# Two-layer hybrid decoder trunk: a one-column product as tensor_scalar, a planner with other prices, and work moved between engines

## The chip, the cores and the metric

The kernel runs on one core of a Trainium2 chip. The metric is the device time of one execution in microseconds; three runs stand for a kernel, and their median is quoted. The engines are TensorE (PE in the profile; PEld is its weight load), VectorE (DVE), ScalarE (ACT), GpSimd (POOL) and SyncE (SP), which issues all DMAs.

## What is computed

Two decoder layers on 1024 tokens of width 1024 in float32, with RMSNorm before and after every sub-layer. Layer 0 mixes with an HGRN2 recurrence (4 heads) beside a chunked gMLP (4 channel groups); layer 1 with dilated sliding-window attention (16 heads). Each layer ends with a squared-ReLU feed-forward of 4096. The parts that the change touches:

```python
def rmsnorm(x, g):
    y = xf * lax.rsqrt(jnp.mean(xf * xf, axis=-1, keepdims=True) + EPS)
    return (y * g.astype(F32)).astype(x.dtype)
...
# gMLP, inside chunks of 128 positions, W_s causal
v = layernorm(v, ln_g, ln_b)
mixed = jnp.einsum('gts,bnsgc->bntgc', w, vb) + b_s.T[None, None, :, :, None]
return u * mixed
...
# HGRN2, per head
o = rmsnorm(o, norm_g.reshape(A_HEADS, A_DV))
o = o.reshape(b_, s_, A_WIDTH) * jax.nn.silu(g)
...
# attention: every head runs (128,1), (512,4), (2048,16) and merges them
mask = (dist >= 0) & (dist <= W) & (k_pos >= 0)
```

## The kernel before, in words

The program is not issued in the order in which it is written. Every call goes to a recorder (Plan.record, Plan.add), which stores it as a numbered operation with its dependences and an estimated cost (Plan.cost). At the end Plan.run replays all operations as a list scheduler: each engine has a queue of what is ready and takes the operation with the lowest number; an operation that becomes ready later runs after its due time. Each engine executes its instructions on the chip in the order that the plan emitted them, so estimated costs decide the order of every queue, but not the work. For VectorE the plan adds a delay where an operation is marked "pair" (two inputs in SBUF) and GpSimd is still busy in the plan. Nearly every instruction of the trace bears line 422, the emitting line; groups are told apart by tile and shape. Tiles come from pools (name "b" in the trace); HT holds activations, WP weights, and mm, tr, pa, pb are banks of PSUM. Values used in products are split in a high and a low part, copied by ScalarE and subtracted by VectorE or GpSimd, and multiplied as three fast products.

The stages, by the trace: input norms and the projection of layer 0 (to about 75 us), HGRN2 heads with the other projections as filling (to 330), output projection and norms (to 475), the first feed-forward product in sixteen blocks (to 780), the second one in four stages of eight chunks (to 1105), attention of layer 1 (to 1575), its output projection (to 1665), and the feed-forward of layer 1 (first product to 2005, second to the end).

The parts that the change touches:

- rstd_act (line 658) and newton (669) compute reciprocal roots on one column per token tile: rstd_act once for every norm of 1024, 64 times in all; newton in three steps, for each of eight tiles of the gMLP norm (one column) and of the HGRN2 head norm (four columns). The last product is a tensor_tensor.
- consts0 (766) prepares constants of layer 0, among them the transposed mixing matrices wsT and the bias, each in a plain form and one with reversed order. lng, lnb and anr are rows broadcast to all partitions.
- gmlp_norm (949) normalizes on VectorE and applies gain and bias on GpSimd (two operations of 128x512 a tile); gmlp_mix (963) multiplies with the mixing matrix and adds the bias on VectorE in two halves.
- onorm (975) multiplies by the root for all four heads at once on VectorE, then by the gain on GpSimd.
- attn_mask (1093) builds a quarter of the attention mask, 256 columns, in a single tile x, with four index generations and sixteen operations on GpSimd and two on VectorE, and stores it to DRAM (maskd); ff2 calls it after chunks 3 to 6 of layer 0. layer1_mix loads the whole mask before attention.
- Attention leaves its output in oTd with the tokens of each tile of 128 in the order (r, u), r being the position modulo 4. reload_oT (1351) restores the order by reading in steps of four.
- ff2 (1572) makes, per chunk, the differences of weight halves on GpSimd (128x1024), splits hidden values and weights on ScalarE and VectorE, two chunks ahead of the products.
- post_end (1761) loads the residual tile, adds the normed result, and stores the tile: in halves for the final output, otherwise at once.

Of the kernel before, what the change touches and what calls it, by code (L numbers as in the profile page):

```python
# [8 lines left out]
F32 = mybir.dt.float32  # L9
# [3 lines left out]
AF = mybir.ActivationFunctionType  # L13
OP = mybir.AluOpType
# [3 lines left out]
P = 128  # L18
D = 1024
# [11 lines left out]
NEG = -1.0e30  # L31
# [145 lines left out]
class Plan:  # L177
# [79 lines left out]
    def add(self, calls):  # L257
# [3 lines left out]
        o["pair"] = any(sum(isinstance(x, View) and x.buf.n not in self.inpsum and x.shape[-1] > 1  # L261
                            for x in list(a)[1:] + [kw.get("in0"), kw.get("in1")]) > 1 for _, _, a, kw in calls)
# [34 lines left out]
    def cost(self, o, eng, meth, a, kw):  # L297
# [31 lines left out]
        return 147 + (2.15 if meth == "tensor_tensor" else 3.3 if meth == "tensor_scalar" else 1.2) * n  # L329
# [14 lines left out]
    def run(self):  # L344
# [81 lines left out]
        while left:  # L426
# [29 lines left out]
            else:  # L456
                end = at + o["cost"]
                if e == "DVE" and o["pair"]:
                    end += min(max(free.get("POOL", 0.0) - at, 0.0), max(o["cost"], 700.0))
# [25 lines left out]
class Trunk:  # L485
# [172 lines left out]
    def rstd_act(self, ss):  # L658
# [7 lines left out]
        nc.vector.tensor_tensor(r, y, z, op=OP.mult)  # L666
        return r

    def newton(self, t, y, n, steps):
        V = self.nc.vector  # L670
        for _ in range(steps):
# [8 lines left out]
            V.tensor_tensor(y2, y, z, op=OP.mult)  # L680
# [85 lines left out]
    def consts0(self, pool):  # L766

        nc, a = self.nc, self.a
        with nc.pool() as tp:
# [36 lines left out]

            ge = tp.tile([P, P], F32, name="ge")
# [7 lines left out]
            for back in range(2):  # L815
# [10 lines left out]
                with nc.group():  # L826
                    for g in range(4):
# [4 lines left out]
                                     bs.strided(P - 1, back3) if back else bs.rearrange("p (g t) -> p g t", g=4), AF.Copy, scale=0.5)  # L832
                self.wsT.append(wt)
                self.bias.append(bias)
        self.lng = self.row(pool, a["b_ln_g"], 512, "lng")
        self.lnb = self.row(pool, a["b_ln_b"], 512, "lnb")
# [112 lines left out]
    def gmlp_norm(self, pool, o, sums):  # L949
# [9 lines left out]
        nc.gpsimd.tensor_tensor(vn, vn, self.lng, op=OP.mult)  # L959
        nc.gpsimd.tensor_tensor(vn, vn, self.lnb, op=OP.add)  # L960
        return vn

    def gmlp_mix(self, t, ob, vn):
# [7 lines left out]
        for i in range(2):  # L971
            part, bias = (x[:, 256 * i:256 * i + 256].rearrange("p (g t) -> p g t", g=2) for x in (tr, self.bias[t % 2]))
            nc.vector.tensor_tensor(ob[t // 4][i][:, :, t % 4 * P:(t % 4 + 1) * P], part, bias, op=OP.add)

    def onorm(self, pool, o):
# [8 lines left out]
        ov = o.rearrange("p (h v) -> p h v", h=4)  # L984
        nc.vector.tensor_tensor(ov, ov, r[:, :, None].to_broadcast([P, 4, P]), op=OP.mult)
        nc.gpsimd.tensor_tensor(o, o, self.anr, op=OP.mult)
# [106 lines left out]
    def attn_mask(self, pool, start):  # L1093


        G = self.nc.gpsimd
        n = 256
        for c0 in (start,):
# [5 lines left out]
            G.tensor_copy(u, d)  # L1104
            G.tensor_scalar(M, u, 128.0, None, op0=OP.is_le)
# [466 lines left out]
    def ff2(self, l, w, a, xmid, xout):  # L1572
# [86 lines left out]
        for m in range(3 * NC):  # L1659
# [27 lines left out]
            if l == 0 and 3 <= m <= 6:  # L1687
                self.attn_mask(prep, 256 * (m - 3))
# [128 lines left out]
```

## Time and profile before

| | |
|---|---|
| median of 3 runs | 2319.9 us (2319.55 to 2323.67) |
| profiled execution, its own time | 2320.68 us |
| its span | 2318.9 us |
| granted TensorE clock, mean | 0.995 |
| VectorE, ScalarE, GpSimd busy | 1616.1, 1114.1, 1097.3 us |
| DMA | 319.10 MB, 138 GB/s |

The span runs from the first to the last instruction; the execution's own time has a little around it. Busy time does not count waits on semaphores, but an engine that is held up inside an instruction counts as busy. A time in brackets behind an instruction is the idle time of its engine before it, with the engine that ended it. The chain of work that ended last runs for 75% of the span through TensorE and for 12% through VectorE.

### The profile page before, as it was taken

To read this page: it belongs to the slowest core of one execution; us is meant where nothing else is said; L and a number is where in the kernel's file an instruction comes from. 1 tells how busy PE (TensorE), PEld (TensorE's weight loads), DVE (VectorE), ACT (ScalarE), POOL (GpSimd) and SP (SyncE) were. 2 spreads that over 40 slices of the span, in tenths; PEclk is the share of its full clock that TensorE was granted. 3 is DMA by queue.
4 is the path that set the end of the run, shared out by engine and by line. 5 is a ranking of instruction groups with operands and counts; after the bars stand their busy time and mean duration, and the time that the engine had idled before them with its cause. 6 is when DMAs were issued, how large, how long until landed. Compare 5 with 4: busy or idle time off the path is not lost.

```text
span 2318.9 us, 32947 instructions
## 1 busy us (share of the span) xinstructions
PE 2259.9 (97%) x11314; PEld 1929.9 (83%) x11314; DVE 1616.1 (70%) x3106; ACT 1114.1 (48%) x2403; POOL 1097.3 (47%) x1184
## 2 busy tenths in 40 slices
PE   8999999999999998999999999998999999999998
PEld 7888778888888787887999999996788888888887
DVE  7688975665555955848888887877765555787746
ACT  6444444442222432435777777787452222433333
POOL 2121453355555889415555555543345555645204
PEclk9999999999999999999999999999999999999999
DMA  5110123334443957754311111114334443877654
GB/s 173 55 35 22 37 82 97 112 111 153 151 150 132 327 203 239 250 206 157 103 46 46 47 46 44 53 43 155 113 132 150 150 151 138 290 277 267 224 176 160
DMA packets 214768, 319.10 MB, mean 138 GB/s; under 512 B 14132, under 2 KB 99144, under 8 KB 214600
## 3 DMA queue, kind: packets, MB, share of 16 engines
q1 hardware_dynamic: 214600, 317.00, 40.5%
q8 instruction: 89, 1.46, 0.3%
q14 instruction: 79, 0.65, 0.1%
HBM read 226.24 MB, written 90.70 MB: 137 GB/s over the span
## 4 chain that ended last, share of the span: by engine, by line
PE 75%; DVE 12%; ACT 4%; POOL 3%; DMA 3%; issue 2%; SPq 0%; DVEq 0%; ACTq 0%; POOLq 0%
PE mm L422 34%; PE pa L422 20%; PE pb L422 13%; PE tr L422 9%; DVE b L422 9%; POOL b L422 3%; ACT b L422 3%; DVE WP L422 2%; DVE HT L422 1%; DMA b<-in_w_ff_dram 1%; DMA b<-in_w_in_odd_dram 1%; DMA b<-oTd 1%; DMA b<-hc 1%; ACT HT L422 0%; ACT WP L422 0%
## 5 line engine op out<-in xcount | busy, mean ns | idle before, releaser
L422 POOL TENSOR_TENSOR b<-b,b 128x512 f32<-128x512 f32 (+4 forms) x500 | 576.4, 1169 | 668.3 <-ACT b L422 324.5
L422 PE MATMUL mm<-WP,HT 128*128 128x512 f32 (+2 forms) x3744 | 822.5, 362 | 3.3 <-DVE HT L422 1.2
L422 PEld LDWEIGHTS mm<-WP,HT 128*128 128x128 f32 x3744 | 655.3, 190 | 82.1 <-DVE HT L422 2.3
L422 ACT ACTIVATE b<-b 128x512 f32<-128x512 f32 (+6 forms) x653 | 327.1, 513 | 369.8 <-POOL b L422 190.0
L422 POOL TENSOR_TENSOR b<-b 128x512 f32<-128x512 f32 (+4 forms) x368 | 331.8, 907 | 352.0 <-DVE b L422 246.0
L422 ACT ACTIVATE WP<-b 128x1024 fp32r<-128x1024 f32 (+2 forms) x248 | 194.3, 792 | 340.2 <-PE pb L422 190.5
L422 DVE TENSOR_TENSOR WP<-b,WP 128x1024 fp32r<-128x1024 f32 (+1 forms) x164 | 225.8, 1385 | 127.9 <-ACT WP L422 127.5
L422 DVE TENSOR_TENSOR b<-b,b 128x1024 fp32r<-128x1024 f32 (+6 forms) x382 | 239.3, 642 | 76.5 <-ACT b L422 58.7
L422 ACT ACTIVATE b<-mm 128x512 f32<-128x512 f32 (+3 forms) x346 | 152.6, 454 | 265.8 <-PE mm L422 246.2
L422 DVE TENSOR_TENSOR HT<-b,HT 128x1024 fp32r<-128x1024 f32 (+3 forms) x131 | 217.9, 1671 | 23.2 <-ACT HT L422 23.0
L422 PE MATMUL tr<-b,b 128*128 128x128 f32 x1074 | 171.1, 278 | 30.2 <-DVE b L422 24.2
L422 PE MATMUL pa<-WP,HT 128*128 128x512 f32 x768 | 193.8, 390 | 0.0
L422 DVE TENSOR_TENSOR b<-tr,b 64x128 fp32r<-64x128 f32 (+5 forms) x404 | 162.7, 407 | 32.8 <-ACT b L422 25.4
L422 PE MATMUL tr<-WP,HT 128*128 128x512 f32 x672 | 171.6, 392 | 7.6 <-DVE b L422 7.3
L422 ACT ACTIVATE HT<-b 128x1024 fp32r<-128x1024 f32 (+4 forms) x147 | 142.6, 973 | 73.8 <-PE mm L422 30.3
L422 PEld LDWEIGHTS tr<-b,b 128*128 128x128 f32 x1074 | 128.9, 147 | 54.1 <-DVE b L422 27.7
L422 PE MATMUL mm<-HT,b 128*128 128x512 f32 x720 | 173.7, 390 | 0.0
L422 PE MATMUL pa<-WP,b 128*128 128x512 f32 x720 | 173.6, 389 | 0.0
L422 DVE TENSOR_TENSOR b<-pa,b 128x512 f32<-128x512 f32 x110 | 75.4, 689 | 135.7 <-PE pa L422 135.6
L422 PEld LDWEIGHTS pa<-WP,HT 128*128 128x128 f32 x768 | 144.2, 188 | 29.9
L422 PEld LDWEIGHTS pa<-WP,b 128*128 128x128 f32 x720 | 134.9, 188 | 27.9
L422 PEld LDWEIGHTS mm<-HT,b 128*128 128x128 f32 x720 | 134.8, 188 | 27.8
(63 smaller groups left out, 3041.1 us busy)
## 6 DMA issues: line engine op xcount, KB each, us to landing
b<-in_w_ff_dram SPq DMA_DIRECT2D x172, 512.0 KB, 4.9
hc<-b SPq DMA_DIRECT2D x224, 256.0 KB, 2.1
b<-hc SPq DMA_DIRECT2D x112, 512.0 KB, 5.6
b<-in_w_in_odd_dram SPq DMA_DIRECT2D x64, 192.0 KB, 2.9
x<-b SPq DMA_DIRECT2D x24, 512.0 KB, 2.7
b<-x SPq DMA_DIRECT2D x24, 512.0 KB, 3.4
b<-in_w_in_even_dram SPq DMA_DIRECT2D x32, 256.0 KB, 2.8
wd<-b SPq DMA_DIRECT2D x16, 512.0 KB, 3.5
```

Of the source, the lines that this page charges most:

```text
L422: return getattr(self.real[eng], meth)(*[x.real() if isinstance(x, View) else x for x in a], **{k: x.real() if isinstance(x, View) else x ...
```

## The change

1. Planner: GpSimd's prices are changed (memset has one of its own); "pair" becomes shares(), which marks any VectorE operation without PSUM that has two inputs, or one input and more than one column of output (a number per partition counts only outside tensor_scalar). The added delay counts a further operation if GpSimd has one ready, and its cap changes.
2. The last product of rstd_act and of newton with one column is a tensor_scalar that takes its second factor as a number per partition.
3. The gMLP norm's gain and bias are no longer applied to the values. The gain becomes a number per partition in the mixing's last step (four scalar_tensor_tensor of 128x128); the bias times the row sums of the mixing matrix, by a product with ones, is added to the bias in the setup. lng and lnb are loaded as 128x4.
4. onorm does both of its products in one scalar_tensor_tensor per head, on VectorE.
5. attn_mask runs on VectorE but for the index generations, and is called after chunks 14, 16, 18 and 20.
6. reload_oT reads and writes plainly; the tokens stay in the order (r, u) in layer 1. post_end therefore loads x2 and stores the result with four DMAs of 32 partitions each (rows_of).

```diff
-        o["pair"] = any(sum(isinstance(x, View) and x.buf.n not in self.inpsum and x.shape[-1] > 1
-                            for x in list(a)[1:] + [kw.get("in0"), kw.get("in1")]) > 1 for _, _, a, kw in calls)
+        o["pair"] = any(self.shares(*c) for c in calls)
...
-        return 147 + (2.15 if meth == "tensor_tensor" else 3.3 if meth == "tensor_scalar" else 1.2) * n
+        if meth == "memset":
+            return 62 + 0.83 * n
+        return 150 + (2.4 if meth == "tensor_tensor" else 4.0 if meth == "tensor_scalar" else 1.2) * n
+
+    def shares(self, eng, meth, a, kw):
+
+        views = [x for x in list(a) + [kw.get("in0"), kw.get("in1")] if isinstance(x, View) and x.shape[-1] > 0]
+        if any(x.buf.n in self.inpsum for x in views) or meth.startswith("dma"):
+            return False
+        out = kw["out"] if "out" in kw else a[0]
+        n = sum(x.shape[-1] > 1 or meth != "tensor_scalar" for x in views if x is not out)
+        return n > 1 or n == 1 and math.prod(out.shape[1:]) > 1
...
-                    end += min(max(free.get("POOL", 0.0) - at, 0.0), max(o["cost"], 700.0))
+                    busy = max(free.get("POOL", 0.0) - at, 0.0)
+                    if busy and now["POOL"]:
+                        busy += o["cost"]
+                    end += min(busy, max(0.85 * o["cost"], 700.0))
...
-        nc.vector.tensor_tensor(r, y, z, op=OP.mult)
+        nc.vector.tensor_scalar(r, y, z, None, op0=OP.mult)
...
-            V.tensor_tensor(y2, y, z, op=OP.mult)
+            if n == 1:
+                V.tensor_scalar(y2, y, z, None, op0=OP.mult)
+            else:
+                V.tensor_tensor(y2, y, z, op=OP.mult)
...
+            self.lng, lnb = pool.tile([P, 4], F32, name="lng"), pool.tile([P, 4], F32, name="lnb")
+            for x, src in ((self.lng, a["b_ln_g"]), (lnb, a["b_ln_b"])):
+                nc.sync.dma_start(x, bass.AP(tensor=src.tensor, offset=src.offset, ap=[[1, P], [P, 4]]))
...
+                tr = self.tr_bank()
+                with nc.group():
+                    nc.tensor.matmul(tr, self.ones.bitcast(F32), wt.rearrange("p g t -> p (g t)"), start=True, stop=True)
+                for g in range(4):
+                    gs = slice(g * P, (g + 1) * P)
+                    nc.vector.scalar_tensor_tensor(bias[:, gs], tr[:, gs], lnb[:, g:g + 1], bias[:, gs], op0=OP.mult, op1=OP.add)
...
-        nc.gpsimd.tensor_tensor(vn, vn, self.lng, op=OP.mult)
-        nc.gpsimd.tensor_tensor(vn, vn, self.lnb, op=OP.add)
...
-            nc.vector.tensor_tensor(ob[t // 4][i][:, :, t % 4 * P:(t % 4 + 1) * P], part, bias, op=OP.add)
+        for g in range(4):
+            gs = slice(g * P, (g + 1) * P)
+            nc.vector.scalar_tensor_tensor(ob[t // 4][g // 2][:, g % 2, t % 4 * P:(t % 4 + 1) * P], tr[:, gs], self.lng[:, g:g + 1],
+                                           self.bias[t % 2][:, gs], op0=OP.mult, op1=OP.add)
...
-        nc.vector.tensor_tensor(ov, ov, r[:, :, None].to_broadcast([P, 4, P]), op=OP.mult)
-        nc.gpsimd.tensor_tensor(o, o, self.anr, op=OP.mult)
+        for h in range(4):
+            hs = slice(h * P, (h + 1) * P)
+            nc.vector.scalar_tensor_tensor(o[:, hs], o[:, hs], r[:, h:h + 1], self.anr[:, hs], op0=OP.mult, op1=OP.mult)
...
-            G.tensor_copy(u, d)
-            G.tensor_scalar(M, u, 128.0, None, op0=OP.is_le)
-            self.nc.vector.tensor_scalar(e, d, 3, None, op0=OP.bitwise_and)
-            G.tensor_scalar(t, e, 0, None, op0=OP.is_equal)
...
+            V.tensor_copy(u, d)
+            V.tensor_scalar(M, u, 128.0, None, op0=OP.is_le)
+            V.tensor_scalar(e, d, 3, None, op0=OP.bitwise_and)
+            V.tensor_scalar(t, e, 0, None, op0=OP.is_equal)
...
-        src = raw.rearrange("p k (r u) -> p k u r", r=4)
-        hi, lo = (self.HT[:, x, k0:k1, ts].rearrange("p k (u r) -> p k u r", r=4) for x in range(2))
-        nc.scalar.activation(hi, src, AF.Copy)
-        (nc.gpsimd if t < LAG["rel"] else nc.vector).tensor_tensor(lo, src, hi.bitcast(F32), op=OP.subtract)
+        hi, lo = (self.HT[:, x, k0:k1, ts] for x in range(2))
+        nc.scalar.activation(hi, raw, AF.Copy)
+        nc.vector.tensor_tensor(lo, raw, hi.bitcast(F32), op=OP.subtract)
+
+    def rows_of(self, x, t, cs, spread):
+
+
+        if not spread:
+            return [(slice(0, P), x[t * P:(t + 1) * P, cs])]
+        return [(slice(32 * r, 32 * r + 32), x[t * P + r:(t + 1) * P:4, cs]) for r in range(4)]
...
-            if l == 0 and 3 <= m <= 6:
-                self.attn_mask(prep, 256 * (m - 3))
+            if l == 0 and m in (14, 16, 18, 20):
+                self.attn_mask(prep, 128 * (m - 14))
...
-        nc.sync.dma_start(x, xin[rows, :])
+        for p, src in self.rows_of(xin, t, slice(0, D), xin is self.x2):
+            nc.sync.dma_start(x[p], src)
...
-                nc.sync.dma_start(xout[rows, d], x[:, d])
+                for p, dst in self.rows_of(xout, t, d, xout is self.out[0]):
+                    nc.sync.dma_start(dst, x[p, d])
```

## Rows read from the trace of the kernel before

**Rows 1.** The page, part 1: busy time, share of the span, instructions

```profile
PE 2259.9 (97%) x11314; PEld 1929.9 (83%) x11314; DVE 1616.1 (70%) x3106; ACT 1114.1 (48%) x2403; POOL 1097.3 (47%) x1184
```

**Rows 2.** Stretches: length, busy time (count) of each engine, TensorE's clock, DMA share, GB/s

```profile
315.00:336.00 21.00, 18.00 (x77) 14.49 (x76) 15.42 (x24) 8.05 (x17) 13.25 (x11) 0.92 0.40 125
783.00:872.00 89.00, 88.68 (x392) 73.08 (x390) 64.33 (x38) 35.33 (x38) 82.26 (x54) 1.00 0.71 249
882.00:970.00 88.00, 86.80 (x383) 71.58 (x382) 59.98 (x42) 31.81 (x32) 66.39 (x41) 1.00 0.75 258
970.00:1048.00 78.00, 78.00 (x346) 64.59 (x345) 45.70 (x42) 26.48 (x30) 13.91 (x6) 1.00 0.56 191
1048.00:1070.00 22.00, 18.63 (x79) 15.03 (x79) 20.53 (x29) 14.79 (x42) 21.60 (x15) 0.92 0.26 92
1100.00:1550.00 450.00, 444.94 (x2751) 422.59 (x2750) 361.74 (x1120) 342.25 (x997) 229.15 (x579) 1.00 0.18 54
1555.00:1665.00 110.00, 97.75 (x476) 78.22 (x475) 84.44 (x168) 78.13 (x164) 42.17 (x44) 0.98 0.43 139
2005.00:2192.00 187.00, 187.00 (x827) 154.65 (x826) 148.12 (x97) 74.58 (x79) 88.96 (x32) 1.00 0.78 270
```

**Rows 3.** TensorE in order of time: start, length, what, idle time before it

```profile
327.60 0.66 PE L422 MATMUL tr<-b,b 128*128 128x128 f32 x4 [3.00 <-POOL b L422]
...
778.66 4.61 PE L422 MATMUL pa<-HT,b 128*128 128x512 f32 x12 [1.85 <-DVE b L422]
...
878.99 2.92 PE L422 MATMUL tr<-WP,HT 128*128 128x512 f32 x6 [7.30 <-DVE b L422]
881.71 1.62 PE L422 MATMUL mm<-WP,HT 128*128 128x512 f32 x6
...
1065.63 0.66 PE L422 MATMUL tr<-b,b 128*128 128x128 f32 x4 [3.37 <-DVE b L422]
```

**Rows 4.** GpSimd's groups by shape: count, busy us, mean ns, idle before

```profile
L422 POOL TENSOR_TENSOR b<-b,b 128x1024 f32<-128x1024 f32 x64 | 180.3, 2818 | 166.6 <-DMA b<-wd 88.1 <-DMA b<-in_w_ff_dram 78.0
...
L422 POOL TENSOR_SCALAR b<-b 128x256 f32<-128x256 f32 x28 | 39.8, 1420 | 1.7
```

**Rows 5.** GpSimd and VectorE in order of time

```profile
238.76 2.65 POOL L422 TENSOR_TENSOR b<-b,b 128x512 f32<-128x512 f32 x2 [27.51 <-DVE b L422]
...
239.98 0.76 DVE L422 TENSOR_SCALAR b<-b 128x1 int32<-128x1 int32 x5
...
775.54 2.47 DVE L422 TENSOR_SCALAR b<-b 128x256 int32<-128x256 int32 x1
...
878.04 0.29 DVE L422 TENSOR_SCALAR b<-b 128x256 int32<-128x256 int32 x1 [6.32 <-POOL b L422]
...
1062.59 1.22 DVE L422 TENSOR_TENSOR b<-b,b 128x1 f32<-128x1 f32 x1
```

**Rows 6.** VectorE's groups by shape

```profile
L422 DVE TENSOR_TENSOR b<-b 128x1 f32<-128x1 f32 x47 | 16.7, 356 | 1.0
...
L422 DVE TENSOR_TENSOR HT<-b,HT 128x512 fp32r<-128x512 f32 x13 | 17.0, 1308 | 4.9 <-ACT HT L422 4.7
...
L422 DVE SCALAR_TENSOR_TENSOR b<-b,b,tr 128x128 f32<-128x128 f32 x24 | 8.7, 361 | 1.7 <-PE tr L422 1.1
```

**Rows 7.** ScalarE's groups by shape

```profile
L422 ACT ACTIVATE WP<-b 128x512 fp32r<-128x512 f32 x72 | 44.2, 625 | 18.9 <-DMA b<-in_w_in_even_dram 9.7 <-PE mm L422 6.1 <-DMA b<-in_w_out_odd_dram 1.3
...
L422 ACT ACTIVATE HT<-b 128x512 fp32r<-128x512 f32 x13 | 15.0, 1154 | 3.8 <-DMA b<-oTd 3.8
```

**Rows 8.** TensorE in order of time, a group of full-precision products

```profile
84.30 0.82 PE L422 MATMUL pa<-b,b 128*128 128x128 f32 x4
```

**Rows 9.** DMA issues: count, KB each, median us from issue to landing

```profile
out_dram<-b SPq DMA_DIRECT2D x16, 256.0 KB, 2.1
...
vd<-b SPq DMA_DIRECT2D x32, 64.0 KB, 1.5
```

**Rows 10.** SP in order of time, two loads behind each other

```profile
0.74 0.87 SPq L422 DMA_DIRECT2D b<-in_x_dram  x2
```

More of the change, by code (lines that the diff above doesn't have):

```diff
@@ L1093, in attn_mask @@
     def attn_mask(self, pool, start):
-        G = self.nc.gpsimd
+        G, V = self.nc.gpsimd, self.nc.vector
         n = 256
@@ L1103, in attn_mask @@
                 G.iota(d[32 * r:32 * r + 32], pattern=[[-1, n]], base=S - P - c0 + r, channel_multiplier=4)
-            G.tensor_copy(u, d)
-            G.tensor_scalar(M, u, 128.0, None, op0=OP.is_le)
-            self.nc.vector.tensor_scalar(e, d, 3, None, op0=OP.bitwise_and)
-            G.tensor_scalar(t, e, 0, None, op0=OP.is_equal)
-            G.tensor_tensor(M, M, t, op=OP.add)
-            G.tensor_scalar(t, u, 512.0, None, op0=OP.is_le)
-            G.tensor_tensor(M, M, t, op=OP.add)
-            G.tensor_scalar(M, M, -1.0, 0.0, op0=OP.add, op1=OP.max)
-            self.nc.vector.tensor_scalar(e, d, 15, None, op0=OP.bitwise_and)
-            G.tensor_scalar(t, e, 0, None, op0=OP.is_equal)
-            G.tensor_tensor(M, M, t, op=OP.add)
-            G.tensor_scalar(t, u, 0.0, None, op0=OP.is_ge)
-            G.tensor_tensor(M, M, t, op=OP.mult)
-            G.tensor_scalar(t, M, 0.0, NEG, op0=OP.is_equal, op1=OP.mult)
-            G.tensor_scalar(u, M, 2.0, LN2_8, op0=OP.is_equal, op1=OP.mult)
-            G.tensor_tensor(t, t, u, op=OP.add)
-            G.tensor_scalar(u, M, 3.0, LN3_8, op0=OP.is_equal, op1=OP.mult)
-            G.tensor_tensor(t, t, u, op=OP.add)
+            V.tensor_copy(u, d)
+            V.tensor_scalar(M, u, 128.0, None, op0=OP.is_le)
+            V.tensor_scalar(e, d, 3, None, op0=OP.bitwise_and)
+            V.tensor_scalar(t, e, 0, None, op0=OP.is_equal)
+            V.tensor_tensor(M, M, t, op=OP.add)
+            V.tensor_scalar(t, u, 512.0, None, op0=OP.is_le)
+            V.tensor_tensor(M, M, t, op=OP.add)
+            V.tensor_scalar(M, M, -1.0, 0.0, op0=OP.add, op1=OP.max)
+            V.tensor_scalar(e, d, 15, None, op0=OP.bitwise_and)
+            V.tensor_scalar(t, e, 0, None, op0=OP.is_equal)
+            V.tensor_tensor(M, M, t, op=OP.add)
+            V.tensor_scalar(t, u, 0.0, None, op0=OP.is_ge)
+            V.tensor_tensor(M, M, t, op=OP.mult)
+            V.tensor_scalar(t, M, 0.0, NEG, op0=OP.is_equal, op1=OP.mult)
+            V.tensor_scalar(u, M, 2.0, LN2_8, op0=OP.is_equal, op1=OP.mult)
+            V.tensor_tensor(t, t, u, op=OP.add)
+            V.tensor_scalar(u, M, 3.0, LN3_8, op0=OP.is_equal, op1=OP.mult)
+            V.tensor_tensor(t, t, u, op=OP.add)
             self.nc.sync.dma_start(self.maskd[:, c0:c0 + n], t)
@@ L1763, in post_end @@
         nc = self.nc
-        rows = slice(t * P, (t + 1) * P)
         x = pl.tile([P, D], F32, name="x", tag="gpre" if last else "x")
-        nc.sync.dma_start(x, xin[rows, :])
+        for p, src in self.rows_of(xin, t, slice(0, D), xin is self.x2):
+            nc.sync.dma_start(x[p], src)
         r = self.rstd_act(ss)
```

5 lines of the change are left out of this document (removed).

## The prediction

> **What bounds the kernel now.** I read the page first: TensorE is busy 2259.9 us, 97% of the span [rows 1], so all of its idle time together is 59 us (2318.9 - 2259.9), and whatever the other engines save can only come back where TensorE waits for them. Next I cut the span into stretches of 25 us and kept those where TensorE idles; the ones that matter here stand in [rows 2]. The reader is to see three: 3.0 us missing between 315 and 336 us (21.00 - 18.00), 3.4 us between 1048 and 1070, and 12.2 us between 1555 and 1665. The granted clock is below 1.00 in all three: part of each stretch ran at 1.2 instead of 2.4 GHz, after the idle time in it, so a gap costs more than its length. Last I looked in TensorE's timeline for who ended each gap [rows 3]: 3.00 us by GpSimd at 327.60; 1.85 us by VectorE at 778.66; 7.30 us by VectorE at 878.99, after which six products took 2.92 us where the next six took 1.62; 3.37 us by VectorE at 1065.63. The same two halves of the feed-forward in layer 1, from 2005 to 2192 us, have no gap at all: TensorE is busy 187.00 of 187.00 us with the same products, and the only thing that layer 0 does besides is the attention mask. That comparison carries most of this prediction.
>
> **The change, part by part.**
>
> *The mask.* It takes 64 operations from GpSimd: 28 comparisons of 1.42 us and 8 like them, 24 sums and 4 conversions, together some 72 us (36 x 1.42 = 51, the rest at about 0.75 us each) [rows 4]. Between 783 and 872 us GpSimd is busy 82.26 of 89 us [rows 2], and it also makes the weight differences of 128x1024, 2.82 us each [rows 4], that the next products need; the gap at 878.99 stands behind a mask step on VectorE that had waited 6.32 us for GpSimd and held up the evacuation queued behind it [rows 5]. Without this, layer 0 should come near layer 1. The loss to be had is 1.85 us of gap at 778.66 and 1.4 us of slow clock behind it (twelve products in 4.61 us, where twice 1.62 are 3.24), 7.30 and 1.3 us at 878.99 (2.92 against 1.62) [rows 3], and 1.2 us that miss between 882 and 970 us [rows 2]: 13.0 us. Added to VectorE are the same 64 operations, 0.29 us each where nothing blocks them [rows 5]: 19 us. They hide in VectorE's idle time, 39 us in layer 1's stretch of 187 us and 32 us between 970 and 1048 us [rows 2]. The four index generations stay on GpSimd; each waits until the previous mask has left its one tile, and the weight differences queue behind it there. The four stores of the mask move with it on SP, and its one reload comes before attention starts; weight loads stand behind them, two chunks ahead, so I cost these at nothing. I take -9.0 us, nearer to layer 1's full pace (-13.0) than to nothing, because the row of layer 1 is the same work without the mask.
>
> *The roots.* 88 small products change their form; 47 of them take 0.356 us on average [rows 6], 1.22 us at worst [rows 5]. For the new form the nearest row is the five one-column steps that took 0.76 us together while GpSimd was running [rows 5]: not blocked. With a pointer I take 0.21 us. Most of it lies beside other work. It pays in the chain before 1065.63, where two such products wait: -2.0 us with the slow clock after it, between 0 and -5 (all of the gap).
>
> The Trainium skill (SBUF - State Buffer, Who interferes with whom) says that a VectorE instruction with two SBUF inputs, and also a tensor_scalar that can run in a two-port mode, is fully blocked while GpSimd holds the shared port. The row of 2.47 us for a mask step that takes 0.29 us alone agrees for 256 columns [rows 5], the five one-column steps do not; by the rule for all of them the roots would bring nothing and the sum would be 2 us less.
>
> *Spatial gating and head norm.* GpSimd loses 24 operations of 128x512, about 1.3 us each (the pair at 238.76 took 2.65) [rows 5]; VectorE gets four pieces of 128x128 instead of two wider ones at the mixing and instead of one at the norm, 0.361 us a piece [rows 6]: at most 0.72 and 1.08 us more for each of eight tiles, I estimate 11 us in all; against it, if half of each 1.3 us was a wait of VectorE, 16 us go with the 24 operations. What ends up on the path is one GpSimd step less in each tile's chain to the transposes, 3.00 us of gap at 327.60 and about 1.5 us of slow clock after it (0.92 over 18 us) [rows 2, 3]: I take -3.5 us, between -4.5 and +1 if VectorE's additions weigh more.
>
> *Setup.* Two products of 128x512 in full precision are added while TensorE has no gap. No row has that shape; four quarter-wide ones took 0.82 us [rows 8], so +1.7 us, between 1.6 and 2.5. Two loads of 512 single numbers replace two broadcast loads of 256 KB on SP; unknown, +0.6 us between -0.8 (the bytes saved) and +3 (two loads of 1.5 us [rows 9] ahead of the first weights).
>
> *Reload of the attention output.* The read in steps of four goes. ScalarE takes 1.154 us with it and 0.625 us for a plain 128x512 [rows 7]; VectorE's 1.308 us [rows 6] should fall by as much. Thirteen full reloads save about 13 us of engine time, in a stretch where TensorE lacks 12.2 us [rows 2]. About a third of that lies on the chains that end gaps: -4.0 us, between 0 and -8. Against it, 24 more loads are issued on SP, 0.45 us apart [rows 10], 1.35 us a tile; the loads of the next tile stand behind them, and this is why I take no more than a third.
>
> *Stores of the result.* 16 become 64. In the last tile the store of the first half is issued when its sum is done, and seven more follow at 0.4 to 0.45 us: the last starts some 2.2 us later than now. It lands sooner, 1.5 us for 64 KB against 2.1 us for 256 KB [rows 9], and the root before it gains 0.1 us (0.356 against 0.21) [rows 6]. So 2.2 - 0.6 - 0.1 = +1.5 us, between 0.8 and 2.2. The earlier stores stand on SP ahead of the last weight loads: +0.6 us, between 0 and 3.
>
> *The planner's prices.* They issue nothing but sort every queue anew. In attention TensorE lacks 5.1 us in 450 [rows 2], so there is little to win: 0, between -3 and +5.
>
> **Sum:** -9.0 - 2.0 - 3.5 + 1.7 + 0.6 - 4.0 + 1.5 + 0.6 = -14.1 us. The profiled execution took 2320.7 us, 1.8 more than its span; it lies 0.8 us above the median of the runs. 2319.9 - 14.1 = 2305.8, say 2306 us.
>
> **Rivals.**
> - *VectorE becomes the bound in layer 0's second feed-forward product* (the slower one). Each of the 64 mask steps costs 0.29 us plus its wait for GpSimd. With GpSimd busy 88.96 of 187 us in operations of 2.8 us, a step that arrives at random waits 0.48 x 1.4 = 0.67 us; 64 x 0.96 = 61 us against 39 us of idle time. If the planner puts all four masks there, TensorE lags 22 us in place of the 13.0 us lost now: 2319.9 - 5.1 + 9 = 2324; at a full microsecond of wait, 44 us, 2346. I put it at 2330. It decides from a wait of 0.31 us. Against it: the steps have late numbers and take only idle slots, GpSimd is busy 13.91 of 78 us from 970 us on, and products run two chunks ahead. 8%.
> - *The order gets worse elsewhere.* The planner now charges VectorE for more waits; if that costs 1% in the 1000 us or so outside the feed-forward, the gain shrinks by 10 us: 2316. For it, only that every queue is sorted anew; against, TensorE's small gaps in attention [rows 2]. 12%.
> - *The roots do not escape the port*: by the rule above, a chain's 0.21 us would still be 1 us now and then: about 2308. 10%.
> - *Everything lands*: layer 0 like layer 1 and two thirds of the reload's gap, -4 and -4 more: 2298. 8%.
>
> **The numbers.** The forecast has 62% and reaches by itself from 2299 to 2314 us. The range of 2296 to 2316 us takes in the third and fourth rivals and part of the second. 0.2% is 4.6 us, about what a measurement of this kernel can tell. Faster by more: 0.62 + 0.10 + 0.08 + 0.02 of the second = 0.82. Within: 0.10, the rest of the second. Slower: 0.08.
>
> **What would show it.** Right: TensorE without a gap between 780 and 970 us, comparisons of 256 columns on VectorE and none on GpSimd, plain reloads near 0.63 us, one-column roots at 0.2 us also beside GpSimd, and 64 result stores, the last some 2 us after the last sum. Wrong: a gap at the change of banks near 870 us that ends on VectorE; SP late with loads behind the fourfold ones near 1600 us; a lower share of TensorE in attention.

## The result and the profile after

The changed kernel takes 2296.6 us (median of four runs, 2293.3 to 2297.7) where the kernel before, timed beside it, takes 2319.8. The ratio worked out from all of these runs is 0.9894, 95% interval 0.9877 to 0.9911 (the medians alone would give 0.9900). That is 23 us faster by the medians and 25 by the ratio (2319.8 x 0.0106); 14 were forecast. The range began at 2296 us, so the time lies at its very edge by the median and just below it by the ratio, 2295. The page of the profiled execution (compare [rows 1]):

```profile
span 2295.6 us, 33048 instructions
PE 2249.6 (98%) x11318; PEld 1926.5 (84%) x11318; DVE 1619.8 (71%) x3218; ACT 1108.8 (48%) x2403; POOL 977.0 (43%) x1096
```

GpSimd lost 120 us of work and VectorE gained 4, as the change says. TensorE's idle time fell from 59 to 46 us and its busy time by 10. Where this happened is seen in stretches that answer to those of [rows 2]; the columns are length, then the busy time (count) of PE, PEld, DVE, ACT, POOL, the granted clock, DMA share and GB/s:

```profile
311.00:332.00 21.00, 20.80 (x96) 16.99 (x95) 13.37 (x26) 9.99 (x19) 10.53 (x9) 1.00 0.39 125
772.00:860.00 88.00, 87.84 (x388) 72.34 (x386) 86.80 (x92) 39.27 (x42) 44.10 (x24) 1.00 0.80 279
860.00:958.00 98.00, 91.99 (x399) 75.80 (x398) 80.26 (x76) 33.37 (x35) 40.85 (x19) 0.97 0.74 256
1036.00:1110.00 74.00, 69.22 (x347) 58.17 (x346) 65.90 (x126) 47.03 (x123) 45.04 (x49) 1.00 0.51 167
1530.00:1640.00 110.00, 101.36 (x503) 82.96 (x503) 73.54 (x180) 74.37 (x179) 41.60 (x44) 0.97 0.45 138
1980.00:2167.00 187.00, 187.00 (x827) 154.84 (x826) 146.63 (x97) 76.09 (x80) 86.41 (x32) 1.00 0.77 269
```

TensorE's timeline (start, length, what, idle time before it and who ended it; compare [rows 3]):

```profile
324.00 0.66 PE L432 MATMUL tr<-b,b 128*128 128x128 f32 x4 [0.20 <-POOL b L432]
866.32 2.93 PE L432 MATMUL tr<-WP,HT 128*128 128x512 f32 x6 [6.01 <-DVE b L432]
1063.20 0.66 PE L432 MATMUL tr<-b,b 128*128 128x128 f32 x4 [0.73 <-DVE b L432]
1099.41 0.44 PE L432 MATMUL tr<-b,b 128*128 128x128 f32 x2 [1.91 <-POOL b L432]
1601.56 0.66 PE L432 MATMUL tr<-b,b 128*128 128x128 f32 x4 [1.71 <-DVE b L432]
```

The gap at the gating (3.00 us) is gone, that at the handover to attention (3.37) is down to 0.73, and that in front of the second product (1.85) is gone. But the largest one, 7.30 us at the change of banks (the start of the second product's second stage, which needs banks that the first stage filled), is still there with 6.01. The prediction had named this gap as a sign of being wrong. VectorE's timeline shows why:

```profile
855.82 2.51 DVE L432 TENSOR_TENSOR b<-b 128x256 f32<-128x256 f32 x1
...
861.16 3.37 DVE L432 TENSOR_TENSOR HT<-b,HT 128x1024 fp32r<-128x1024 f32 x1
864.45 1.21 DVE L432 TENSOR_TENSOR WP<-b,WP 128x1024 fp32r<-128x1024 f32 x1
865.59 0.68 DVE L432 TENSOR_TENSOR b<-tr,b 128x512 f32<-128x512 f32 x1
...
867.92 1.86 DVE L432 CAST b<-b 128x256 f32<-128x256 int32 x1
...
872.02 0.68 DVE L432 TENSOR_TENSOR b<-pa,b 128x512 f32<-128x512 f32 x1
```

The evacuations that free the banks (those that read tr and pa) now stand behind and between mask steps on a VectorE that is busy 86.80 of the 88 us up to 860; a few sums of the mask take 2.51 us beside GpSimd, where most of the same shape take 0.42.

The groups by shape, with count, busy us and mean ns (compare [rows 6, 7]): plain reloads on VectorE and ScalarE, the one-column steps, and the mask's steps.

```profile
L432 DVE TENSOR_TENSOR HT<-b,HT 128x512 fp32r<-128x512 f32 x13 | 9.3, 722 | 6.3 <-ACT HT L432 6.3
L432 ACT ACTIVATE HT<-b 128x512 fp32r<-128x512 f32 x13 | 8.2, 629 | 8.0 <-DMA b<-oTd 8.0
L432 DVE TENSOR_SCALAR b<-b 128x1 f32<-128x1 f32 x268 | 50.8, 197 | 41.2 <-ACT b L432 36.8
L432 DVE TENSOR_SCALAR b<-b,b 128x1 f32<-128x1 f32 x76 | 18.3, 243 | 7.0 <-ACT b L432 5.9
L432 DVE TENSOR_TENSOR b<-b 128x256 f32<-128x256 f32 x32 | 19.7, 617 | 0.7
L432 DVE TENSOR_SCALAR b<-b 128x256 f32<-128x256 f32 x28 | 9.9, 367 | 0.6
```

The end, SP and VectorE in order of time. The last 24 stores are issued on SP within 11.80 us, 0.49 us each:

```profile
2281.42 11.80 SPq L432 DMA_DIRECT2D out_dram<-b  x24
```
```profile
2288.83 1.41 DVE L432 SCALAR_TENSOR_TENSOR b<-b,b,b 128x512 f32<-128x512 f32 x2
```

The last sum ends at 2290.24 and the span at 2295.6; TensorE ended at 2285.42, 10.2 us before the end, where it was 7.85 before.

### The profile page after: what moved, and what is told of

Its sections match the earlier page's. It is cut to its first block, busy times and chain, and to the rows that moved or that the text cites. A ratio compares the mean times of both kernels' runs of the same rounds, so it can differ in the third digit from the quotient of the medians.

```text
span 2295.6 us, 33048 instructions
## 1 busy us (share of the span) xinstructions
PE 2249.6 (98%) x11318; PEld 1926.5 (84%) x11318; DVE 1619.8 (71%) x3218; ACT 1108.8 (48%) x2403; POOL 977.0 (43%) x1096
## 5 line engine op out<-in xcount | busy, mean ns | idle before, releaser
L432 POOL TENSOR_TENSOR b<-b,b 128x512 f32<-128x512 f32 (+4 forms) x477 | 537.5, 1143 | 756.6 <-ACT b L432 319.6
L432 POOL TENSOR_TENSOR b<-b 128x512 f32<-128x512 f32 (+4 forms) x343 | 303.2, 892 | 359.3 <-DVE b L432 291.9
L432 DVE TENSOR_TENSOR b<-b,b 128x128 f32<-128x128 f32 (+5 forms) x331 | 215.9, 670 | 66.9 <-ACT b L432 59.6
L432 DVE TENSOR_TENSOR HT<-b,HT 128x1024 fp32r<-128x1024 f32 (+3 forms) x131 | 195.7, 1500 | 21.0 <-ACT HT L432 20.9
L432 DVE TENSOR_TENSOR b<-tr,b 64x128 fp32r<-64x128 f32 (+4 forms) x388 | 157.0, 407 | 39.2 <-ACT b L432 32.0
L432 ACT ACTIVATE HT<-b 128x1024 fp32r<-128x1024 f32 (+4 forms) x147 | 134.4, 916 | 75.0 <-DMA b<-hc 38.0
L432 ACT ACTIVATE b<-tr 64x128 fp32r<-64x128 f32 (+3 forms) x376 | 134.5, 360 | 53.7 <-PE tr L432 46.3
```

What stands on the lines that cost most here:

```text
L432: return getattr(self.real[eng], meth)(*[x.real() if isinstance(x, View) else x for x in a], **{k: x.real() if isinstance(x, View) else x ...
```

## Experiments

The gain came out too large in stretches for which I had costed nothing: 4 us by the first feed-forward, 7 around attention. The first question was whether the planner's order makes them. Times below are medians. A ratio is always to the kernel before, timed beside the run, with its 95% interval; the changed kernel has 0.9894. Runs whose intervals overlap are not told apart.

**Planner alone, operations alone.** The first kernel is the one before with the diff's planner lines only; the second the changed one with these taken back.

```diff
-        o["pair"] = any(sum(isinstance(x, View) ...
+        o["pair"] = any(self.shares(*c) for c in calls)
-        return 147 + (2.15 if ... else 3.3 if ...
+        return 150 + (2.4 if ... else 4.0 if ...
-                    end += min(max(free.get("POOL", 0.0) - at, 0.0), max(o["cost"], 700.0))
+                    ...
+                    end += min(busy, max(0.85 * o["cost"], 700.0))
```

> The kernel before with the planner's four edits alone (prices of GpSimd, the rule of what shares the port, the surcharge on VectorE); no operation is added or removed. Theory A (the order is the missing gain: the stretches of HGRN and attention, 4 and 8 us shorter than I allowed for, come from it): 10 to 13 us faster than before, 2307 to 2310 us. Theory B (the order brings nothing, every part of the gain comes from an operation that was changed): within 3 us of before, 2317 to 2323 us.

> The changed kernel with the planner's prices of before. Theory A: it loses what the order brought, 2306 to 2310 us, about where the prediction stood. Theory B: within 3 us of the changed kernel, 2294 to 2300 us. A third outcome, slower than 2312 us, would say that the new operations need the new prices to be placed at all.

Measured: 2293.1 us (0.9892, 0.9878 to 0.9905) and 2302.1 us (0.9925, 0.9912 to 0.9939). The order alone brings 26.7 us, more than either theory had it. The operations alone bring 17.7, and in the new order they bring nothing: 2293.1 without them, 2296.6 with them, ratios 0.9892 and 0.9894. The two don't add up: behind the changed operations the new order is worth 5.5 us (2302.1 - 2296.6) and not 26.7. How far each one is from the kernel before at the same products (minus is ahead; starts by TensorE's timeline, us; last, the span). These are single profiled executions, the fastest of their runs for the order alone and the operations alone, so their last row shows 1.6 and 3.4 us more than the medians:

| start of | before | changed | order alone | operations alone |
|---|---|---|---|---|
| HGRN | 69.31 | +3.4 | -0.3 | +1.7 |
| first transposes after 290 us | 327.60 | -3.6 | -6.7 | -3.9 |
| feed-forward 1, layer 0 | 463.57 | -7.9 | -10.7 | -7.9 |
| feed-forward 2, layer 0 | 784.48 | -11.8 | -12.3 | -7.0 |
| attention's first 128x384 | 1108.85 | -18.3 | -23.2 | -17.3 |
| feed-forward 1, layer 1 | 1689.40 | -25.4 | -28.2 | -23.0 |
| feed-forward 2, layer 1 | 2006.90 | -24.8 | -27.6 | -22.9 |
| span | 2318.9 | -23.3 | -28.3 | -21.1 |

From the second feed-forward product to attention the changed operations, the moved mask and the roots, bring 10.3 us in the old order (17.3 - 7.0), the new order 10.9 with the mask still on GpSimd, and both together only 6.5. The moved mask does in the old order what the prediction said: TensorE has no gap of more than 0.16 us there, in a stretch in which the changed kernel loses 6.01 (the operations alone, columns as in the stretches above):

```profile
777.00:877.00 100.00, 99.84 (x440) 82.32 (x439) 91.20 (x105) 40.19 (x43) 50.27 (x30) 1.00 0.76 260
877.00:975.00 98.00, 98.00 (x434) 81.14 (x433) 76.86 (x66) 36.60 (x37) 37.52 (x14) 1.00 0.78 265
```

How an order alone removes most of the same gap is seen on VectorE at the change of banks. First the kernel before, in which the mask step of [rows 5] waits at 878.04 and the evacuations come after it; the step before that had waited 12.31 us:

```profile
866.75 0.29 DVE L422 TENSOR_SCALAR b<-b 128x256 int32<-128x256 int32 x1 [12.31 <-POOL b L422]
...
878.25 0.68 DVE L422 TENSOR_TENSOR b<-tr,b 128x512 f32<-128x512 f32 x1
...
879.98 0.68 DVE L422 TENSOR_TENSOR b<-tr,b 128x512 f32<-128x512 f32 x1
...
881.71 1.28 DVE L422 TENSOR_TENSOR b<-pa,b 128x512 f32<-128x512 f32 x2
```

Then the order alone, with the same operations:

```profile
850.89 0.68 DVE L432 TENSOR_TENSOR b<-tr,b 128x512 f32<-128x512 f32 x1
...
852.69 0.69 DVE L432 TENSOR_TENSOR b<-tr,b 128x512 f32<-128x512 f32 x1
...
855.95 0.68 DVE L432 TENSOR_TENSOR b<-pa,b 128x512 f32<-128x512 f32 x1
869.67 0.29 DVE L432 TENSOR_SCALAR b<-b 128x256 int32<-128x256 int32 x1 [13.04 <-POOL b L432]
869.88 0.68 DVE L432 TENSOR_TENSOR b<-pa,b 128x512 f32<-128x512 f32 x1
```

The mask step waits for GpSimd even longer, 13.04 us, but three of the four evacuations stand ahead of it now; only the last is caught, and TensorE loses 3.08 us there instead of 7.30 and the slow clock behind it.

**Which lines of the planner.** The kernel before with the rule of shares() alone, the prices alone, the surcharge alone, and rule with prices; and a control with the prices moved the other way.

```diff
-        return 147 + (2.15 if meth == "tensor_tensor" else 3.3 if meth == "tensor_scalar" else 1.2) * n
+        return 144 + (1.9 if meth == "tensor_tensor" else 2.6 if meth == "tensor_scalar" else 1.2) * n
```

> The kernel before with one planner edit: which VectorE operations count as held up by GpSimd (now also those with one wide input, and none that reads PSUM), old prices and old surcharge. Theory R (the rule is what the new order rests on): 15 to 27 us faster than before, 2293 to 2305 us. Theory J (each of the three edits corrects a part): 5 to 12 us, 2308 to 2315 us. Theory L (the order of before was an unlucky one, any new sorting gives the gain): 15 to 27 us faster here and in the three runs beside it.

> The kernel before with GpSimd's prices alone changed (2.15 to 2.4 and 3.3 to 4.0 ns a column). Theory R: within 5 us of before. Theory J: 5 to 12 us faster. Theory L: 15 to 27 us faster.

> The kernel before with the surcharge alone changed: a held-up VectorE operation is charged a second time its cost where GpSimd has more work ready. Theory R: within 5 us of before. Theory J: 5 to 12 us faster. Theory L: 15 to 27 us faster.

> A control: the kernel before with GpSimd's prices moved by the same amount to the other side (2.15 to 1.9 and 3.3 to 2.6 ns a column), further from the durations in the trace. Theories R and J: within 5 us of before, or slower. Theory L: 10 us faster or more, since this sorts the queues anew as well.

> The kernel before with the rule and GpSimd's prices, but the old surcharge. Alone they brought 9.1 and 11.3 us, and the surcharge alone cost 4.8; the four edits together 26.7. Theory J (parts that add up): 2298 to 2302 us, and the surcharge brings the rest, 5 to 8 us, only where the rule and the prices tell it rightly when GpSimd is busy. Theory K (the surcharge is a loss here too): below 2293 us. Theory S (the edits are substitutes, each corrects the same stalls): 2306 us or more.

Measured: rule 2311.0 us (0.9956, 0.9941 to 0.9971), prices 2308.9 (0.9949, 0.9932 to 0.9966), surcharge 2324.9 (1.0022, 1.0013 to 1.0031), control 2318.6 (0.9994, 0.9984 to 1.0003), rule and prices 2298.2 (0.9910, 0.9893 to 0.9927). So 9.1 and 11.3 us alone and 21.8 together: they add up. The surcharge loses 5 us alone; on top of the other two it brings 5 by the medians, but those intervals overlap. The two other new sortings, the control and the surcharge alone, bring nothing or a loss, which speaks against an order of before that was just an unlucky one. This is theory J, each edit a part.

The place of the mask step can be read in each of these runs. With the prices alone all four evacuations stand ahead of the step that waits, and TensorE has no gap at the change of banks:

```profile
859.60 0.68 DVE L424 TENSOR_TENSOR b<-tr,b 128x512 f32<-128x512 f32 x1
...
864.67 0.68 DVE L424 TENSOR_TENSOR b<-tr,b 128x512 f32<-128x512 f32 x1
865.27 1.27 DVE L424 TENSOR_TENSOR b<-pa,b 128x512 f32<-128x512 f32 x2
...
881.47 0.29 DVE L424 TENSOR_SCALAR b<-b 128x256 int32<-128x256 int32 x1 [13.79 <-POOL b L424]
```

In the other four a step that has waited for GpSimd stands ahead of them, and the gap there is 12.06 us in the control, 10.42 with the surcharge, 5.04 with the rule and 4.52 with rule and prices. So the place of the step goes with the gap, but nearer prices alone don't fix the place: with the rule added it is ahead again. Nor is the place the whole gain: from the second product to attention the prices alone bring 4.2 us (a new gap of 3.40 us stands at 956.00), and the rest of the 26.7 us, before this stretch and around attention, was not traced to single operations.

**The operations one by one, in the new order.** Each is the changed kernel with one part of the diff taken back: the mask on GpSimd and at its old place; the reload in steps of four with plain rows; setup, gating and head norm; the roots.

> The changed kernel with the attention mask back on GpSimd, at its four early numbers. Theory A of the mask (the landmarks: 3.9 us by the start of the second product's second stage, 0.9 and 1.1 us after it): 5 to 7 us slower than the changed kernel, 2302 to 2304 us, with a gap near 770 us. Theory B (the prediction's -9.0 us was right and something else gave back 3 us): 8 to 10 us slower. Theory C (the gap near 866 us would be there without any mask): 1 to 3 us slower.

> The changed kernel with the reload of the attention output in steps of four again, and with it plain rows in layer 1's loads and in the stores of the result. The landmarks give -4.0 us between attention and the second half of layer 1, and +2.4 us at the end: by these it is 1.6 us slower, 2297 to 2300 us, and its tail from TensorE's last product is 7.9 us instead of 10.2. If the reload brought more, and part of it was lost to loads queued on SP, 2301 us or more.

> The changed kernel with the setup, the gating norm, the mixing and the head norm of before. By the landmarks the setup is 3.4 us longer in the changed kernel and 0.3 us shorter with the new prices alone: if that is these parts' price, and the order alone already gives what they were to give, this is 3 to 5 us faster than the changed kernel, 2291 to 2294 us. By the prediction's terms (-3.5 for the gating, +2.3 for the setup) it is 1 us slower, 2297 to 2299 us.

> The changed kernel with the last product of each reciprocal root as a product of two tiles again. By the prediction's term 2 us slower, 2298 to 2300 us, at most 5. Rival: with the new order these products no longer stand in a chain that ends a wait of TensorE, and it is within 1 us of the changed kernel.

Measured: old mask 2298.8 us (0.9908, 0.9895 to 0.9922), old reload 2295.3 (0.9896, 0.9883 to 0.9910), old gating and setup 2291.1 (0.9878, 0.9864 to 0.9893), old roots 2293.3 (0.9887, 0.9872 to 0.9902). All intervals overlap with the changed kernel's, so no part is shown to be worth anything here. By the medians the differences are 2 to 6 us; the mask's 2.2 is below the 8 to 10 us of the prediction and the 5 to 7 of the landmarks, but the intervals are too wide to rule out the latter. From the second product to attention this run gains 3.9 us on the kernel before and the order alone 10.9, with the same mask in the same place and the same planner: what is sorted around the mask moves this stretch by 7 us. Two terms can be read in place. With the old setup HGRN starts at 69.14 us instead of 72.74: the setup costs 3.6 us (1.7 in the old order, by the table of starts). With the old reload the end is 7.8 us behind TensorE instead of 10.2: the fourfold stores cost 2.4 us; and the stretch from attention to layer 1's feed-forward gains 3.9 us on the kernel before (it starts 23.0 ahead and ends 26.8) instead of 7.1. The order alone, with the old reload, gains 5.0 there (28.2 - 23.2), so sorting is in this difference too.

A part put back sorts every queue anew, so these totals hold sorting too. For the roots this can be taken out: the old products, told to the planner at the new form's price.

```diff
-        nc.vector.tensor_scalar(r, y, z, None, op0=OP.mult)
+        nc.vector.tensor_tensor(r, y, z, op=OP.mult)
...
+            if meth == "tensor_tensor" and n == 1:
+                return 63 + 0.52 * n + 62
...
+        if meth == "tensor_tensor" and math.prod(out.shape[1:]) == 1:
+            return False
```

> The changed kernel with the roots' last products as products of two tiles, but told to the planner at the price and rule of the new form, so that every queue keeps the order of the changed kernel. What differs is the operation alone. If the operation is worth what the prediction said: 1 to 3 us slower than the changed kernel, 2298 to 2300 us. If the 3.3 us that the changed kernel lost against old roots sorted anew are the operation's own: 2 to 4 us faster, 2293 to 2295. If they were sorting: within 1.5 us of the changed kernel.

Measured: 2294.9 us (0.9889, 0.9875 to 0.9904), 1.7 us below the changed kernel and inside its interval. The 88 products in the old form, by VectorE's groups:

```profile
L436 DVE TENSOR_TENSOR b<-b 128x1 f32<-128x1 f32 x54 | 13.6, 253 | 1.1
L436 DVE TENSOR_TENSOR b<-b,b 128x1 f32<-128x1 f32 x34 | 12.3, 361 | 0.8
```

The new form does save VectorE time: one-column steps take 69.1 us in all in the changed kernel (50.8 + 18.3 in the groups above), and 77.2 here (these 25.9, and 51.3 in the two groups of tensor_scalar). The time of the kernel doesn't show these 8 us.

**How far sorting alone moves the time.** The order alone, with GpSimd's prices moved a little further; later as far as the trace has them.

```diff
-        return 150 + (2.4 if meth == "tensor_tensor" else 4.0 if ...
+        return 150 + (2.5 if meth == "tensor_tensor" else 4.2 if ...
```

> A control beside the first run: the kernel before with the new planner and GpSimd's prices moved a little (2.4 to 2.5 and 4.0 to 4.2 ns a column). It shows how far a new sorting alone moves a kernel whose prices are about right. If it is within 2 us of the first run's 2293.1 us, the differences of 3 to 5 us between the kernels with new prices belong to the parts that were put back; if it is 3 to 8 us off, to sorting, and only runs in one order can price a part.

> The kernel before with the new planner and GpSimd's prices at what the trace of before shows: 2.6 ns a column makes 2.81 us of a sum of 1024 columns (measured 2.818), 4.6 makes 1.33 us of a comparison of 256 columns (measured 1.420); the new prices make 2.61 and 1.17 of them. If the nearer price is the better order, as the last step (2.4 to 2.5, 6.2 us faster) would have it: 2284 to 2288 us. If that step was scatter of the sorting: anywhere between 2286 and 2298 us, above 2289 telling for scatter.

Measured: 2286.9 us (0.9860, 0.9845 to 0.9874) and 2288.9 us (0.9860, 0.9846 to 0.9875). The first is not the neutral control that I called it, since it moves the prices towards the trace. For a sum of 1024 columns that takes 2.82 us and a comparison of 256 that takes 1.42 [rows 4]:

| planner's price of the two, us | surcharge and rule | time, us |
|---|---|---|
| 2.09, 0.81 | old | 2318.6 |
| 2.35, 0.99 (before) | old | 2319.8 |
| 2.61, 1.17 | old | 2308.9 |
| 2.61, 1.17 | new | 2293.1 |
| 2.71, 1.23 | new | 2286.9 |
| 2.81, 1.33 | new | 2288.9 |

Nearer prices give the better order up to the last step, where the ratio stays at 0.9860 (2 us more by the medians): that step tells nothing. The step before it, 6.2 us for a tenth of a nanosecond a column, can be nearer prices or scatter of the sorting; no run separates the two. In the run with 2.71 the change of banks has no gap at all, with the mask untouched on GpSimd at its old place; the stretch from the first feed-forward product to 925 us, then VectorE:

```profile
456.00:925.00 469.00, 469.00 (x2106) 388.53 (x2105) 294.96 (x284) 165.81 (x209) 322.83 (x222) 1.00 0.56 194
```
```profile
850.75 0.68 DVE L432 TENSOR_TENSOR b<-tr,b 128x512 f32<-128x512 f32 x1
...
854.22 0.68 DVE L432 TENSOR_TENSOR b<-pa,b 128x512 f32<-128x512 f32 x1
856.64 0.69 DVE L432 TENSOR_TENSOR b<-pa,b 128x512 f32<-128x512 f32 x1 [1.74 <-PE pa L432]
...
871.19 0.29 DVE L432 TENSOR_SCALAR b<-b 128x256 int32<-128x256 int32 x1 [8.01 <-POOL b L432]
```

All four evacuations stand ahead of the step that waits 8.01 us.

**A faster kernel from these parts.** The order alone with the mask on VectorE in the first half of the feed-forward (eight pieces of 128 columns); the same with the plain reload and half of the last tile's stores on ScalarE's queue; the changed kernel with one transfer for each four; and all that seemed to help, with 2.5 and 4.2.

```diff
+                if l == 0 and 3 <= i < 11 and (i - 3) % 1 == 0:
+                    self.attn_mask(pl, 128 * ((i - 3) // 1), 128)
```
```diff
-                for p, dst in self.rows_of(xout, t, d, xout is self.out[0]):
-                    nc.sync.dma_start(dst, x[p, d])
+                for n, (p, dst) in enumerate(self.rows_of(xout, t, d, xout is self.out[0])):
+                    (nc.scalar if last and n % 2 else nc.sync).dma_start(dst, x[p, d])
```
```diff
-        return [(slice(32 * r, 32 * r + 32), x[t * P + r:(t + 1) * P:4, cs]) for r in range(4)]
+        y = x[t * P:(t + 1) * P, cs]
+        return y.rearrange("(u r) c -> r u c", r=4) if spread else y
```

> The kernel before with the new planner and the mask moved to VectorE and to the first half of the feed-forward, in pieces of 128 columns, where VectorE is busy 12 to 17 of 25 us and TensorE 25.00 of 25.00. If the mask still costs 2 to 6 us in the second half of layer 0 (gaps near 768 and 855 us): 2287 to 2291 us. If the gap at the change of banks there stands without a mask: 2291 to 2294 us.

> The same with the plain reload, the fourfold loads of layer 1's rows and the fourfold stores, of which the last tile's go out half on SP and half on ScalarE's queue. The reload brought 4.0 us before the second half of layer 1, the fourfold stores took 2.4 back at the end; with two queues the last store is issued some 1.6 us earlier: 2 to 4 us faster than the run beside it. If the reload's gain was sorting: within 1 us of it.

> The changed kernel with each fourfold load of layer 1's rows and each fourfold store of the result as one transfer over the same rows. If the tail is bound by issues on SP: the last store starts about 1.8 us earlier, lands some 0.4 us later, and the kernel is 1.5 to 2.5 us faster, 2294 to 2295 us, the stretch from TensorE's last product to the end 8 to 9 us instead of 10.2. If the rows themselves (512 numbers each, four rows apart) are what makes them slow: no change.

> The new planner with 2.5 and 4.2 ns a column, the early mask on VectorE and the plain reload with the last stores on two queues; roots, gating and setup of before. If the gains of these add up (6.2 us of the prices to the 2288.5 of the kernel without them): 2282 to 2285 us. If each only sorts anew: 2285 to 2292 us.

Measured: early mask 2289.6 us (0.9868, 0.9853 to 0.9882), with plain reload 2288.5 (0.9866, 0.9850 to 0.9883), one transfer 2322.8 (1.0015, 1.0005 to 1.0024; 26 us above the changed kernel, see the last section), all together 2292.9 (0.9878, 0.9861 to 0.9894). The early mask leaves TensorE busy 88.00 of 88 and 98.00 of 98 us in the second half (772 to 860 and 860 to 958 us); in the first half 1.3 us are missing, where the order alone misses 1.9. The plain reload and its stores change 1.1 us, which is not told from nothing, and two queues don't shorten the end: TensorE ends at 2272.96, 11.4 us before it, and SP's own stores end 4.7 us behind the last sum (3.0 in the changed kernel); why was not followed. What helped singly doesn't add up: the last kernel lies 6 us above the run with moved prices alone, though the intervals just overlap. The fastest of the eighteen by its median is that one, the kernel before with the new planner and 2.5 and 4.2 ns a column, 2286.9 us: 9.7 us below the changed kernel, and the intervals to the kernel before (0.9845 to 0.9874, 0.9877 to 0.9911) don't meet.

## Why the prediction was wrong

The sign was right and the size was not. The step that failed is the last term of the sum, "The planner's prices": "They issue nothing but sort every queue anew. In attention TensorE lacks 5.1 us in 450, so there is little to win: 0, between -3 and +5." The runs put 26.7 us in its place with the old operations, and 5.5 behind the changed ones, which is the base that the sum adds it to. The other terms, 14.1 us in all, measured 17.7 in the old order; so the 9.1 us that the forecast missed are 5.5 of the planner and 3.6 of the operations.

I had looked for bad order where TensorE's gaps are small and many, in attention, and had read the large gaps as too much work on GpSimd. [Rows 5] held the other reading: an operation of 0.29 us that waits 6.32 us in an in-order queue, with an evacuation behind it, is a fault of place, and the planner put it there with a price for GpSimd's sums of 2.35 us where [rows 4] have 2.82; with the prices alone changed the step stands behind the evacuations and the gap is gone. I had both numbers and did not divide them. Both readings were right about the same gap: less work removes it (the operations alone) and a better place removes it (the prices alone), and what was missing is that both together don't pay twice.

By terms, against the landmarks (the starts in the table):

- *Mask* (-9.0): 10.3 us from the second product to attention, roots included, where the old order is kept, so the size was near. "Layer 0 should come near layer 1" came true with the mask moved in the old order (197.84 of 198 us busy) and without moving it in the run with moved prices; it failed in the changed kernel, which has both. The first rival's picture, a VectorE that is full (86.80 of 88 us), is seen there: the 64 steps took some 36 us instead of 19 (by shape 9.9, 6.6, 4.9 and 24 of 617 ns), 0.57 each; that is 0.28 above 0.29, near the 0.31 from which I had it decide, and a part of it is no wait, since the sums take 0.42 alone. But the steps took some 34 us with the operations alone too, without a gap, so their sum does not explain the gap: there the first evacuation starts at 862.60, before TensorE needs the bank, and in the changed kernel at 865.59, more than 5 us behind the need.
- *Roots* (-2.0): not seen; within 2 us of nothing in one and the same order. The gap at 1065.63 did shrink, but to 1.67 us in the order alone, where the roots are old, and only to 2.86 with the operations alone, where they are new. The Trainium skill (SBUF - State Buffer, Who interferes with whom) has a tensor_scalar blocked where it can run in a two-port mode; the trace agrees for 256 columns (three of them take 0.82 us alone and 3.01 at worst). The one-column steps were not blocked, as forecast (0.197 us on average of 268).
- *Gating and head norm* (-3.5): HGRN and gating together gained 7.0 us in the changed kernel, 6.4 with the order alone and 5.6 with the operations alone. The 4.3 us between gating and feed-forward were not in the sum at all: three gaps of 0.75 us are among them, and either the order or the operations remove them (4.0 and 4.1 us). This is the largest part of what the operations brought beyond the forecast.
- *Setup* (+2.3 with its loads): 3.6 us in the new order, 1.7 in the old one.
- *Reload* (-4.0): 3.2 us by the run with the old one, with sorting in it; ScalarE's 0.629 us is the duration forecast and VectorE's 0.722 is near it (1.308 less the same 0.53).
- *Stores* (+2.1 with those ahead of the last weights): 2.4 us, of which 1.9 lie behind the last sum (5.4 us to the end instead of 3.5). That SP's issues make them is argued from 24 stores in 11.80 us; the run with one transfer could not test it, because that transfer is slow itself.
- The rival "the order gets worse elsewhere" had the right place, every queue sorted anew, and the wrong sign; in the changed kernel the operations and the order overlap, which no case of mine held.

What stays open: why the changed operations, worth 17.7 us in the old order, bring nothing in the new one. Setup and end cost 6 us there, but the spread of sorting is as large, and only the roots were priced in one order.

## What to carry to other kernels

Where a planner or a hand-written order sorts in-order queues, compare its prices with the trace before costing anything else: if they are off by a fifth, as here, a gap of TensorE may be an operation's place and not its work, and the sign of it is a short operation that waits long with an evacuation behind it. Gains of a better order and of less work that remove the same wait don't add up; try each alone. And where every edit sorts the queues anew, a part of a few microseconds is priced only in one fixed order.

## What was not expected of the hardware

One transfer that takes four interleaved groups of rows is far slower than four transfers of one group each. In the changed kernel with one transfer, VectorE waits for the row loads at the end, and after its last sum, at 2307.50 us, 13.0 us pass to the end of the span (2320.5) instead of 5.4:

```profile
2301.99 1.41 DVE L432 SCALAR_TENSOR_TENSOR b<-b,b,b 128x512 f32<-128x512 f32 x2 [6.12 <-DMA b<-x]
...
2306.08 1.42 DVE L432 SCALAR_TENSOR_TENSOR b<-b,b,b 128x512 f32<-128x512 f32 x2
```

The core's 16 DMA engines are busy 0.22 of this time on average (the column before the last):

```profile
2307.00:2320.50 13.50, 0.00 (x0) 0.00 (x0) 0.50 (x1) 0.00 (x0) 0.00 (x0) 0.50 0.22 85
```

TensorE also waits 7.62 us at 1583.33, behind reloads of the attention output that are late; that the row loads beside them make them late is likely and was not shown:

```profile
1583.33 9.77 PE L432 MATMUL mm<-WP,HT 128*128 128x512 f32 x30 [7.62 <-ACT HT L432]
```

And what a gap costs after its end differs between runs, each seen in one execution. In the kernel with all that helped, a wait of 4.29 us at 1100.78 is followed by ten microseconds at half clock, 1.2 GHz (a second wait of 1.75 us falls into them); columns as in the stretches above:

```profile
1100.00:1105.00 5.00, 2.47 (x11) 2.29 (x12) 4.64 (x11) 1.20 (x2) 1.37 (x7) 0.50 0.28 97
1105.00:1110.00 5.00, 5.00 (x20) 4.90 (x21) 3.96 (x12) 3.32 (x12) 0.19 (x2) 0.50 0.11 30
```

With moved prices alone a wait of 4.16 us in the same place, at 1093.98, is followed by some three at half clock, and by 1100 us it is full again:

```profile
1094.00:1097.00 3.00, 3.00 (x11) 3.00 (x12) 2.90 (x8) 1.65 (x5) 1.56 (x2) 0.59 0.52 174
1097.00:1100.00 3.00, 3.00 (x19) 2.96 (x18) 2.75 (x9) 0.27 (x2) 0.00 (x0) 0.84 0.65 238
```

By an estimate from these stretches, half of TensorE's busy time at the lower level, the half clock costs 3.7 us in the first run and 1.7 in the second; a few microseconds between two orders can come from this.
